# Weight tiles split whole, partial sums put back into PSUM, and wider adaLN tiles in a float32 decoder block

## The chip, the cores and the metric

The kernel runs on one core of one Trainium2 chip. The metric is the device time of one execution in microseconds. A core has TensorE (PE in the profile, with PEld for its weight loads), VectorE (DVE), ScalarE (ACT), GpSimd (POOL), SyncE (SP, which here issues nearly all loads) and 16 DMA engines.

## The reference

One decoder layer over 256 tokens of width 2048, all in float32. What matters of it:

```python
mod = silu(c) @ ada_w + ada_b                    # 2048 -> 6 x 2048
sh1, sc1, g1, sh2, sc2, g2 = split(mod, 6)
h = rms_norm(x, mix_pre_g) * (1 + sc1) + sh1
q, k, v, a, g = split(h @ w_in)                  # 1024 columns each
attn = causal_attention(q, k, v)                 # 8 heads of 128; one block of 256 keys
u = silu(layer_norm(causal_depthwise_conv(a * sigmoid(g), 31 taps)))
y = concat(attn, u) @ w_out
x = x + g1 * rms_norm(y, mix_post_g)
h = rms_norm(x, ffn_pre_g) * (1 + sc2) + sh2
y = (silu(h @ w_gate) * (h @ w_up)) @ w_down     # hidden width 5632
x = x + g2 * rms_norm(y, ffn_post_g)
```

## The kernel before

**Products in three parts.** Every large product is made of fp32r matmuls. A weight tile of 1 MB (4 blocks of 128 rows by 512 columns, name `raw`) is loaded from HBM; ScalarE rounds it into a high tile `wh` (line 610, or 630 where two column groups share a load), and VectorE subtracts that from the tile and keeps the rest as a low tile `wl` (line 611 or 631). The activations exist as a high and a low tensor too, and PE adds three products: high by high, low weight by high, high by low. A `raw` tile is split in two operations of 1024 columns per engine, into tiles of 4 KB per partition, of which there are five high and five low.

**Two forms.** In `multiply_all` (line 656) a job that is `side` (line 668, matmuls on line 674) holds 128 weight columns still and moves 256 token columns, so that its result has channels on partitions. Else (`mm`, lines 680 to 682) 128 tokens are held still, once for each of two token halves `t`, and 512 weight columns move. Before the change the q, k, a and g parts of w_in and all of gate and up are `side`; v, w_out and w_down are not. A unit of PE work is two K blocks of one token half.

**Stages.** `chunks` cuts the 16 K blocks of the first normalisation: for each chunk the adaLN scale and shift (SC1, SH1) are made, `h_chunk` (line 534) turns and scales x into `h0` and `h1`, and then come those w_in products that `cuts` lets end with this chunk. A product cut into parts keeps its sum in SBUF: `put` (line 709) copies the first part out with ScalarE and adds each later part with VectorE (line 717). Then come attention, the convolution (`conv`, line 759; 6 of 8 channel tiles go through ScalarE, lines 786 to 791), a layer norm, w_out in two parts, the second normalisation (`h2_chunk`, line 1113), and the feed-forward part in three passes of 4, 3 and 4 groups of 512 hidden columns. The first pass runs gate and up in four K parts (`fcuts`).

**adaLN.** `ada` (line 453) makes 128 to 512 columns of one of the six vectors from tiles of 1 MB (96 in all), either on PE (line 476, mode 'p'), on VectorE (lines 485 and 487, mode 'd'), or on the one that the plan finds free (mode 'a'). PE then sums over partitions (line 518) or spreads the row (line 512).

**Order.** Nothing is ordered by the chip's arrival order. `Plan` simulates the engines at build time with a cost and a priority (`pri`) for each task and writes the resulting order down, one queue per engine. Loads are picked in `pick_dma` from a queue of weights and a queue of adaLN tiles; the `before` and `after` numbers say at which weight load an adaLN tile must or may go. At most two weight loads whose split isn't done run ahead (`nw`):

```python
if a is not None and (w is None or a["before"] <= w["i"]):
    pick = "a" if a_ok else None
elif w_ok and ahead < nw:
    pick = "w"
elif a_ok and a["after"] <= w["i"]:
    pick = "a"
```

Where PE has nothing to do, the plan gives it small matmuls (line 422) that keep it active. Buffers are named pools: `raw` has 5 tiles of 8 KB, `t2` (512-column scratch) 3, PSUM four banks `pa` for the large products and four banks `pt` for the rest.

## Time and profile before

| | |
|---|---|
| median of 3 runs | 1223.05 us (1222.06 to 1223.63) |
| the profiled execution | 1223.58 us, span 1221.8 us, mean granted clock 0.993 |
| PE busy | 1196.4 us (98% of the span) |
| DVE busy | 877.6 us (72%) |
| ACT busy | 599.7 us (49%) |
| DMA | 307.71 MB, mean 252 GB/s |

The span runs from the first to the last instruction. The time of an execution has a little outside the span. Matmuls are pipelined, so that the length of one in the profile is more than the distance from one to the next; PE's pace is read from the starts.

### The profile page before, as it was taken

How to read it: one execution, taken by the hardware profiler on the slowest of the kernel's cores; microseconds unless marked ns; L12 is line 12 of the kernel's file. 1: busy time of each engine (PE TensorE's matmuls, PEld its weight loads, DVE VectorE, ACT ScalarE, POOL GpSimd, SP SyncE). 2: the span in 40 equal slices, each digit the busy share in tenths (PEclk: the TensorE clock that was granted, in tenths of full speed). 3: DMA queues.
4: the chain of work that ended last, by engine and by line, in shares of the span. 5: the costliest groups of instructions: out<-in, count | busy, mean ns of one | idle time of the engine just before them, and what ended most of it. 6: DMA issues, size and time to landing. Idle time of an engine off the chain costs nothing.

```text
span 1221.8 us, 19898 instructions
## 1 busy us (share of the span) xinstructions
PE 1196.4 (98%) x8275; PEld 1072.2 (88%) x8275; DVE 877.6 (72%) x1121; ACT 599.7 (49%) x860; POOL 16.2 (1%) x29
## 2 busy tenths in 40 slices
PE   5999999999999989999999999999999999999997
PEld 4899799997558769999998789999988999999886
DVE  4799889999978789998788996444555455455554
ACT  3643344998965465534454344434433444444441
POOL 1000000000000010000000000000000000000000
PEclk9999999999998999999999999999999999999999
DMA  9999996558997989988558997655556555555532
GB/s 334 343 341 340 370 348 207 177 179 302 343 383 253 326 315 375 323 297 274 173 185 324 365 363 254 196 174 179 198 175 192 187 173 184 195 173 179 200 104 69
DMA packets 160507, 307.71 MB, mean 252 GB/s; under 512 B 5244, under 2 KB 21920, under 8 KB 159648
## 3 DMA queue, kind: packets, MB, share of 16 engines
q1 hardware_dynamic: 159520, 304.11, 72.5%
q0 software_dynamic: 544, 2.11, 0.5%
q8 instruction: 65, 1.06, 0.4%
q10 hardware_dynamic: 352, 0.21, 0.1%
q14 instruction: 26, 0.21, 0.0%
HBM read 304.32 MB, written 2.10 MB: 251 GB/s over the span
## 4 chain that ended last, share of the span: by engine, by line
PE 89%; ACT 4%; DMA 3%; DVE 1%; issue 1%; SPq 1%; POOL 0%; POOLq 0%; DVEq 0%; ACTq 0%
PE pa L674 54%; PE pa L680 10%; PE pa L682 10%; PE pa L681 10%; PE pt L476 3%; DMA raw<-in_ada_w_dram 2%; ACT prod L788 2%; ACT wh L610 1%; PE pt L518 1%; DMA xt<-in_x_dram 1%; DVE t L487 1%; PE pt L512 1%; SPq L626 0%; DVE wl L611 0%; PE pt L825 0%
## 5 line engine op out<-in xcount | busy, mean ns | idle before, releaser
L674 PE MATMUL pa<-h,wh 128*128 128x256 f32 x3840 | 701.6, 284 | 0.0
L611 DVE TENSOR_TENSOR wl<-raw,wh 128x1024 fp32r<-128x1024 f32 x372 | 451.3, 1223 | 271.8 <-ACT wh L610 270.8
L610 ACT ACTIVATE wh<-raw 128x1024 fp32r<-128x1024 f32 x372 | 392.6, 1060 | 498.0 <-PE pa L674 291.1
L674 PEld LDWEIGHTS pa<-h,wh 128*128 128x128 f32 x3840 | 593.9, 188 | 6.4 <-issue 2.7
L674 PE MATMUL pa<-h,wl 128*128 128x256 f32 x1920 | 540.9, 282 | 0.0
L674 PEld LDWEIGHTS pa<-h,wl 128*128 128x128 f32 x1920 | 363.9, 190 | 0.5 <-issue 0.2
L487 DVE SCALAR_TENSOR_TENSOR t<-raw,cact,t 128x512 f32<-128x512 f32 (+1 forms) x238 | 160.9, 676 | 7.6 <-DVE stats L832 0.3
L680 PE MATMUL pa<-wh,hid 128*128 128x512 f32 x352 | 140.9, 400 | 0.0
L682 PE MATMUL pa<-wh,hid 128*128 128x512 f32 x352 | 139.6, 397 | 0.0
L681 PE MATMUL pa<-wl,hid 128*128 128x512 f32 x352 | 139.6, 397 | 0.0
L681 PEld LDWEIGHTS pa<-wl,hid 128*128 128x128 f32 x352 | 66.4, 189 | 16.5 <-issue 0.7
L680 PEld LDWEIGHTS pa<-wh,hid 128*128 128x128 f32 x352 | 66.4, 189 | 16.5 <-issue 0.7
L682 PEld LDWEIGHTS pa<-wh,hid 128*128 128x128 f32 x352 | 66.4, 189 | 16.1
L788 ACT ACTIVATE prod<-conv,taps 128x256 f32<-128x256 f32 x180 | 74.9, 504 | 0.2 <-DVE conv L791 0.2
L791 DVE TENSOR_TENSOR conv<-conv,prod 128x1536 f32<-128x1536 f32 x30 | 52.6, 1753 | 2.1 <-ACT prod L788 1.9
L476 PE MATMUL pt<-raw,cpad 128*32 128x512 f32 (+1 forms) x384 | 45.7, 571 | 5.5 <-DMA raw<-in_ada_w_dram 5.4
L476 PEld LDWEIGHTS pt<-raw,cpad 128*32 128x32 f32 x384 | 9.1, 114 | 21.7 <-issue 10.0
L680 PE MATMUL pa<-wh,mixa 128*128 128x512 f32 x64 | 28.0, 438 | 0.0
L680 PE MATMUL pa<-wh,h 128*128 128x512 f32 x64 | 26.9, 421 | 0.0
L682 PE MATMUL pa<-wh,mixa 128*128 128x512 f32 x64 | 26.3, 412 | 0.0
L681 PE MATMUL pa<-wl,mixa 128*128 128x512 f32 x64 | 26.3, 410 | 0.0
L774 DVE SCALAR_TENSOR_TENSOR conv<-conv,taps 128x256 f32<-128x256 f32 x60 | 25.7, 480 | 0.0
(154 smaller groups left out, 786.5 us busy)
## 6 DMA issues: line engine op xcount, KB each, us to landing
raw<-in_ada_w_dram SPq DMA_DIRECT2D x96, 1024.0 KB, 7.4
raw<-in_w_gate_dram SPq DMA_DIRECT2D x44, 1024.0 KB, 5.3
raw<-in_w_up_dram SPq DMA_DIRECT2D x44, 1024.0 KB, 5.2
raw<-in_w_down_dram SPq DMA_DIRECT2D x44, 1024.0 KB, 5.1
raw<-in_w_in_dram SPq DMA_DIRECT2D x32, 1024.0 KB, 6.8
raw<-in_w_out_dram SPq DMA_DIRECT2D x16, 1024.0 KB, 7.9
raw<-in_w_in_dram SPq DMA_DIRECT2D x16, 512.0 KB, 7.4
xt<-in_x_dram SPq DMA_DIRECT2D x2, 1024.0 KB, 10.1
```

Of the source, the lines that this page charges most:

```text
L476: nc.tensor.matmul(ps.t[32 * (k % 4):32 * (k % 4) + 32, 0:wd], cpad[:, k0 + k, :], view()[:, k, :], start=me == mine[0] and k < 4, stop=me ...
L487: nc.vector.scalar_tensor_tensor(acc.t[:, 0:wd], view()[:, k, :], s, acc.t[:, 0:wd], op0=ALU.mult, op1=ALU.add)
L512: a = add("PE", 0.86, min(prio, pri["cap"]), lambda: nc.tensor.matmul(pt.t, ones, acc.t, start=True, stop=True), [a], [pt, acc])
L610: a = add("ACT", 0.475 * m, p, lambda raw=raw, u=u, m=m, wh=wh: nc.scalar.activation(wh.t[:, 0:m, :], raw.t[:, u:u + m, :], AF.Copy), [loa ...
L611: b = add("DVE", 0.567 * m, p, lambda raw=raw, u=u, m=m, wh=wh, wl=wl: nc.vector.tensor_sub(wl.t[:, 0:m, :], raw.t[:, u:u + m, :], f32(wh. ...
L674: nc.tensor.matmul(job.ps[t].t[:, 256 * n:256 * n + 256], w.t[:, j, cs], h, start=u == 0 and j == r and n == 0 and i == 0, stop=end and j ...
L680: nc.tensor.matmul(job.ps[t].t, hi, wh.t[:, j, :], start=u == 0 and j == r, stop=False)
L681: nc.tensor.matmul(job.ps[t].t, hi, wl.t[:, j, :], start=False, stop=False)
L682: nc.tensor.matmul(job.ps[t].t, lo, wh.t[:, j, :], start=False, stop=end and j == r + len(ks) - 1)
L774: nc.vector.scalar_tensor_tensor(cacc[:, k, :], upad[:, k, i:i + 256], w, cacc[:, k, :], op0=ALU.mult, op1=ALU.add)
L788: nc.scalar.activation(T("prod")[:, i % 2, k, :], upad[:, k, i:i + 256], AF.Copy, scale=w)
L791: pa = add("DVE", 0.267 * CFG["nact"] + 0.07, pri["conv"] + 0.001 * i, lambda i=i: nc.vector.tensor_add(cacc[:, nv:], cacc[:, nv:], T("pro ...
```

## The change

It has these parts.

- A `raw` tile is split in one operation of up to 2048 columns per engine (`split`), into three high and two low tiles of 8 KB per partition.
- A job that continues a sum in SBUF (`base`) no longer adds behind its matmuls. ScalarE copies the sum back into the job's PSUM bank ahead of them, and they accumulate on it. `put` always copies with ScalarE. The last part of a sum is then used straight from PSUM: the sigmoid and the product of the gated units, SiLU and product of gate and up, the squares and the gain of y.
- Gate and up are no longer `side`. Their product has tokens on partitions, so `up_evac` turns it with four PE transposes per 512 columns and token half.
- adaLN pieces can be 1024 columns wide: a tile of 1 MB then holds 2 K blocks of 1024 columns, and a piece holds two scratch tiles. The pieces are listed in `s2`, `g1` and `g2` and in `chunks`.
- The settings in `CFG` are others: cuts, chunks, modes, priorities, load positions, 5 convolution tiles on ScalarE instead of 6, the second token half of x from weight load 3 on instead of 1.

```diff
 CFG = {'raw': 5,
- 'wh': 5,
- 'wl': 5,
+ 'wh': 3,
+ 'wl': 2,
...
- 'x1_before': 1,
+ 'x1_before': 3,
  'uni': 2,
- 'g1_before': 23,
- 'c_before': (-192, -5, 77, 198),
+ 'g1_before': 126,
...
- 'pri': {'conv': 10.889,
-         'att': 1.269,
-         'g1': 2.484,
-         's2': 2.504,
-         'g2': 8.462,
-         'cap': 1.455,
-         'ln': 2.276,
-         'glu': 6.517,
-         'h': 0.32,
-         'turn': 7.06,
-         'hid': 8.565,
-         'h2': 2.033},
+ 'pri': {'conv': 28.181,
+         'att': 0.346,
+         'g1': 1.434,
+         's2': 7.314,
+         'g2': 2.213,
+         'cap': 0,
+         'ln': 2.918,
+         'glu': 0.2,
+         'h': 0,
+         'hid': 0,
+         'h2': 0.821,
+         'base': 4.302,
+         'turn': 1.115},
  'silu': 1,
- 'h1': 'DADDDADA',
- 'h2': 'DADDAAAA',
+ 'h1': 'DADDADAD',
+ 'h2': 'DAADADDD',
...
- 'nact': 6,
- 'stagger': 4,
- 'stagger1': 4,
- 'joint': 2,
+ 'nact': 5,
+ 'stagger': 7,
+ 'stagger1': 8,
+ 'joint': 1,
...
- 'fcuts': (0, 4, 8, 12, 16),
- 'mode': {1: 'pdap', 0: 'daad', 2: 'papp', 4: 'padd', 3: 'dpdd', 5: 'dddd'},
- 'chunks': (0, 2, 4, 6, 8, 12, 16),
- 'cuts': ((0, 2, 6, 12, 16), (0, 2, 6, 16), (0, 4, 6, 8, 16)),
+ 'fcuts': (0, 4, 8, 16),
+ 'mode': {1: 'pdaa', 0: 'ppdp', 2: 'daap', 4: 'pada', 3: 'paap', 5: 'dadp'},
+ 'chunks': (0, 2, 4, 8, 16),
+ 'cuts': ((0, 2, 4, 8, 16), (0, 4, 8, 16), (0, 8, 16)),
  'parts': ((0, 1, 2, 3), (4, 5, 6), (7, 8, 9, 10)),
- 'g1_from': 51,
- 'c_after': (50, 119, -180, -13),
- 'g2_from': 0}
+ 'g1_from': 1,
+ 'c_after': (-9, 103, -49, 33),
+ 'g2_from': 0,
+ 's2': ((0, 4), (4, 8), (8, 16)),
+ 'g1': ((0, 8), (8, 16)),
+ 'g2': ((0, 8), (8, 16)),
+ 'inj': 1}
...
-    wh_pool = Slots([sbt([P, 2, 512], "wh%d" % i, F32R) for i in range(CFG["wh"])])
-    wl_pool = Slots([sbt([P, 2, 512], "wl%d" % i, F32R) for i in range(CFG["wl"])])
+    wh_pool = Slots([sbt([P, 4, 512], "wh%d" % i, F32R) for i in range(CFG["wh"])])
+    wl_pool = Slots([sbt([P, 4, 512], "wl%d" % i, F32R) for i in range(CFG["wl"])])
...
+        c0, c1 = kbs
         n = c1 - c0
-        wd = P * n
+        mode = CFG["mode"][m][c0 // 4]
+        nc2 = max(1, n // 4)
+        wd = P * min(n, 4)
         per = 16 // n
-        acc = Buf(ac_pool)
+        acc = [Buf(t2_pool) for _ in range(1 if mode == "p" else nc2)]
...
+                    strips = 4 // nc2
                     for k in range(per):
-                        nc.tensor.matmul(ps.t[32 * (k % 4):32 * (k % 4) + 32, 0:wd], cpad[:, k0 + k, :], view()[:, k, :],
-                                         start=me == mine[0] and k < 4, stop=me == mine[-1] and k >= per - 4,
-                                         tile_position=(0, 32 * (k % 4)), skip_group_check=True)
+                        for h in range(nc2):
+                            o = 32 * (k % strips + strips * h)
+                            nc.tensor.matmul(ps.t[o:o + 32, 0:wd], cpad[:, k0 + k, :], view()[:, k, wd * h:wd * h + wd],
+                                             start=me == mine[0] and k < strips, stop=me == mine[-1] and k >= per - strips,
+                                             tile_position=(0, o), skip_group_check=True)
...
+                        for h in range(nc2):
+                            w = view()[:, k, wd * h:wd * h + wd]
+                            if me == mine[0] and k == 0:
+                                nc.vector.tensor_scalar(acc[h].t[:, 0:wd], w, s, None, op0=ALU.mult)
+                            else:
+                                nc.vector.scalar_tensor_tensor(acc[h].t[:, 0:wd], w, s, acc[h].t[:, 0:wd], op0=ALU.mult, op1=ALU.add)
+            dve = 0.2 + 0.178 * per + 0.00111 * per * wd if nc2 == 1 else 2.75
...
+            pts = [Buf(pt_pool) for _ in range(nc2)]
+            o = m * D + P * c0
+            a = plan.fetch(prio, lambda: nc.gpsimd.dma_start(br.t[0:64 * nc2 - 63:64, :], ada_b[:, o:o + P * n].rearrange("o (h n) -> (o h) n", n=512)), [prev], 0.01, [br])
...
+            def spread():
+                for h in range(nc2):
+                    if all_pe() and nc2 == 2:
+                        nc.tensor.matmul(pts[h].t, sel[:, h:h + 1].to_broadcast([P, P]), acc[0].t, start=True, stop=True)
+                    else:
+                        nc.tensor.matmul(pts[h].t, ones, acc[h].t, start=True, stop=True)
+            a = add("DVE", 0.602 * nc2, prio, bias, [a], [br] + acc)
+            a = add("PE", 0.86 * nc2, min(prio, pri["cap"]), spread, [a], pts + acc)
...
+    def split(load, raw, n):
+
+        wh, wl = Buf(wh_pool), Buf(wl_pool)
+        p = 1.0 + 1e-4 * nw[0]
+        a = add("ACT", 0.02 + 0.465 * n, p, lambda: nc.scalar.activation(wh.t[:, 0:n, :], raw.t[:, 0:n, :], AF.Copy), [load], [raw, wh])
+        b = add("DVE", 0.07 + 0.533 * n, p, lambda: nc.vector.tensor_sub(wl.t[:, 0:n, :], raw.t[:, 0:n, :], f32(wh.t[:, 0:n, :])), [a], [raw, wh, wl])
+        plan.queue(load, plan.wq, {"t": load, "i": nw[0], "end": b})
+        nw[0] += 1
+        return wh, wl, b
...
             load = add("DMA", 0.728 * n, 0, fetch, bufs=[raw])
+            wh, wl, b = split(load, raw, n)
             for u in range(0, n, 2):
-                m = min(2, n - u)
...
+                units.append((kbs[i + u:i + min(u + 2, n)], wh, wl, b, range(u, min(u + 2, n))))
...
+        for i, (units, job) in enumerate(pairs):
+            if job.base is not None and CFG["inj"]:
+                for t in range(NT):
+                    place, deps = job.base(t)
+                    last[i][t] = add("ACT", 0.48, pri["base"], lambda job=job, t=t, place=place: nc.scalar.activation(job.ps[t].t, place(), AF.Copy),
+                                     deps + begun[-1], [job.ps[t]])
+            begun.append([])
...
+                loose = job.base is not None and bool(CFG["inj"])
...
                         for i, (w, h) in enumerate(((wh, hi), (wl, hi), (wh, lo))):
-                            nc.tensor.matmul(job.ps[t].t[:, 256 * n:256 * n + 256], w.t[:, j, cs], h, start=u == 0 and j == r and n == 0 and i == 0,
-                                             stop=end and j == r + len(ks) - 1 and n == 1 and i == 2)
...
+            last[i][t] = add("PE", (0.72 if job.side else 0.705) * len(ks), 3.0, side if job.side else mm, deps, [wh, wl, job.ps[t]])
+            if u == 0:
+                begun[base + i].append(last[i][t])
...
-    def put(dst, job, last, first, prio=0.0, more=()):
-
-        last = [[x] + list(more) for x in last]
-        ts = []
-        for t in range(NT):
-            if first:
-                ts.append(add("ACT", 0.48, prio, lambda t=t: nc.scalar.activation(dst(t), job.ps[t].t, AF.Copy), last[t], [job.ps[t]]))
-            else:
-                ts.append(add("DVE", 0.602, prio, lambda t=t: nc.vector.tensor_add(dst(t), dst(t), job.ps[t].t), last[t], [job.ps[t]]))
-        return ts
+    def put(dst, job, last, prio=0.0, more=()):
+
+        return [add("ACT", 0.48, prio, lambda t=t: nc.scalar.activation(dst(t), job.ps[t].t, AF.Copy), [last[t]] + list(more), [job.ps[t]]) for t in range(NT)]
+
+    def base_of(place, made, key):
+
+        if key not in made:
+            return None
+        tasks = made[key]
+        return lambda t: (lambda: place(t), [tasks[t]])
...
         def f(job, last):
-            AGD[kind, j] = put(lambda t: pair(T("ag")[:, kind], 2 * j + t), job, last, first)
-            if fin and kind == 1:
-                glu(j)
+            if not fin:
+                AGD[kind, j] = put(ag_place(kind, j), job, last)
+            elif kind == 1:
+                SIG[j] = [add("ACT", 0.48, pri["glu"], lambda t=t: nc.scalar.activation(ag_place(1, j)(t), job.ps[t].t, AF.Sigmoid), [last[t]], [job.ps[t]]) for t in range(NT)]
+            else:
+                for t in range(NT):
+                    ct = 4 * j + 2 * t
+                    U[ct] = U[ct + 1] = add("DVE", 0.69, pri["glu"], lambda t=t, ct=ct: nc.vector.tensor_mul(
+                        upad[:, ct:ct + 2, HALO:], job.ps[t].t.rearrange("p (k n) -> p k n", k=2), T("ag")[:, 1, ct:ct + 2, :]), [last[t], SIG[j][t]], [job.ps[t]])
         return f
...
+    def y_evac(y, junk, part, cg, fin, base, gdep):
+
+        d = y_place(y, cg)
...
             if not fin:
+                YP[y, cg] = put(d, job, last, more=PVD if y is y1 and part == 0 else ())
...
+                a = add("ACT", 0.61, 0.1, lambda t=t, o=o: nc.scalar.activation(T(junk)[:, t, :], job.ps[t].t, AF.Square, scale=ROOT, accum_out=stats[:, o:o + 1]), [last[t]], [job.ps[t]])
+                b = add("DVE", 0.69, 0.15, lambda t=t: nc.vector.tensor_mul(d(t), job.ps[t].t, gain[:, 512 * cg:512 * cg + 512]), [last[t], gdep[cg]], [job.ps[t]])
...
                 z, ga = GATE[g][t]
...
+                a = add("DVE", 0.69, 0.0, lambda t=t, z=z: nc.vector.tensor_mul(z.t, z.t, job.ps[t].t), [last[t], ga], [job.ps[t], z])
...
+                pt = Buf(pt_pool)
+
+                def turn(z=z, pt=pt):
+                    for k in range(4):
+                        nc.tensor.transpose(pt.t[:, P * k:P * k + P], z.t[:, P * k:P * k + P], ident)
+                a = add("PE", 0.434, pri["turn"], turn, [a], [z, pt])
 
                 def part(s, t=t):
-                    return pair(T("hid%d" % s), 2 * slot + t)
-                h = add("ACT", 0.48, pri["hid"], lambda z=z, part=part: nc.scalar.activation(part(0), z.t, AF.Copy), [a], [z])
-                l = add("DVE", 0.602, pri["hid"], lambda z=z, part=part: nc.vector.tensor_sub(part(1), z.t, f32(part(0))), [h], [z])
+                    return T("hid%d" % s)[:, 4 * slot:4 * slot + 4, P * t:P * t + P]
+                h = add("ACT", 0.48, pri["hid"], lambda pt=pt, part=part: nc.scalar.activation(part(0), pt.t.rearrange("p (k n) -> p k n", k=4), AF.Copy), [a], [pt])
+                l = add("DVE", 0.602, pri["hid"], lambda pt=pt, part=part: nc.vector.tensor_sub(part(1), pt.t.rearrange("p (k n) -> p k n", k=4), f32(part(0))), [h], [pt])
                 HID[slot][t] = [h, l]
+                PARTD.append(last[t])
...
-        return Job(pa_pool, h_stat, h1_deps, (ag_evac if kind >= 3 else qkv_evac)(kind % 3, j, k0 == 0, k1 == KB), kind != 2)
+        evac, place, made = (ag_evac, ag_place, AGD) if kind >= 3 else (qkv_evac, qkv_place, QKV)
+        kind %= 3
+        return Job(pa_pool, h_stat, h1_deps, evac(kind, j, k1 == KB), (evac, kind) != (qkv_evac, 2), base_of(place(kind, j), made, (kind, j)))
...
+        for k0 in range(c0, c1, 4):
+            outs = h_chunk(k0, min(k0 + 4, c1), sd, pri["h"], outs, [(0,), (1,)] if c0 == 0 and CFG["x1_before"] else [(0, 1)])
...
+    G1D = [e for ks in CFG["g1"] for e in ada(G1, ks, n1 + CFG["g1_before"], CFG["g1_from"], pri["g1"], [gl])]
...
+    S2D = []
+    for i, ks in enumerate(CFG["s2"]):
+        at = n1 + nout + 2 * nc_ * (max(x for x in CFG["fcuts"] if x <= ks[0]) // 4)
+        fr = n1 + nout + CFG["c_after"][i]
+        S2D += [[ada(m, ks, at + CFG["c_before"][i], fr, pri["s2"]) for m in (SC2, SH2)]] * ((ks[1] - ks[0]) // 4)
...
         for k0, k1 in zip(fc, fc[1:]) if n0 else ():
...
+                ev = part_evac(i) if k1 < KB else up_evac(g, i // 2) if i % 2 else gate_evac(g)
+                weights(w, 0, 512 * g, list(range(k0, k1)), Job(pa_pool, h2_stat, h2_deps, ev, base=part_base(i)))
...
+            weights(w_gate, 0, 512 * g, list(range(KB)), Job(pa_pool, h2_stat, h2_deps, gate_evac(g)))
+            weights(w_up, 0, 512 * g, list(range(KB)), Job(pa_pool, h2_stat, h2_deps, up_evac(g, slot)))
```

## Rows read from the trace of the kernel before

**Rows 1.** The page: engines, busy us, share of the span, instructions.

```profile
PE 1196.4 (98%) x8275; PEld 1072.2 (88%) x8275; DVE 877.6 (72%) x1121; ACT 599.7 (49%) x860; POOL 16.2 (1%) x29
```

**Rows 2.** The chain that ended last, longest pieces: start us, us, what.

```profile
745.54 125.27 PE pa L674 x1044
...
938.27 184.32 PE pa L674 x1536
```

**Rows 3.** Order of time, all engines, start of the kernel.

```profile
8.82 5.62 SPq L626 DMA_DIRECT2D raw<-in_w_in_dram  x1
...
14.49 0.65 SPq L445 DMA_DIRECT2D xt<-in_x_dram  x1
...
25.81 1.91 ACT L448 ACTIVATE ag<-xt 128x2048 f32<-128x2048 f32 x1 [0.54 <-DMA xt<-in_x_dram]
...
32.66 1.94 PE L476 MATMUL pt<-raw,cpad 128*32 128x256 f32 x16
34.53 0.58 PE L674 MATMUL pa<-h,wh 128*128 128x256 f32 x1
```

**Rows 4.** Stretches: length, busy us of PE, PEld, DVE, ACT, POOL, granted clock, DMA share, GB/s.

```profile
214.00:280.00 66.00, 65.94 (x490) 62.63 (x489) 63.90 (x89) 65.75 (x144) 0.00 (x0) 1.00 0.56 191
280.00:384.00 104.00, 102.91 (x542) 68.20 (x542) 91.81 (x136) 79.12 (x172) 2.18 (x4) 0.97 0.90 323
```

**Rows 5.** Order of time between w_out and gate.

```profile
444.12 0.69 DVE L1142 TENSOR_TENSOR h<-t,h 128x512 fp32r<-128x512 f32 x1
...
448.96 0.37 PE L674 MATMUL pa<-h,wh 128*128 128x256 f32 x1
```

**Rows 6.** Order of time behind the last matmul.

```profile
1212.58 0.69 DVE L717 TENSOR_TENSOR y<-y,pa 128x512 f32<-128x512 f32 x1 [0.19 <-PE pa L682]
1213.31 0.60 ACT L954 ACTIVATE pa<-y 128x512 f32<-128x512 f32 x1 [4.89 <-DVE y L717]
```

**Rows 7.** Order of time, PE: first w_down matmul of the last run, first instruction behind it.

```profile
1122.43 0.40 PE L680 MATMUL pa<-wh,hid 128*128 128x512 f32 x1
...
1212.38 2.17 PE L422 MATMUL pt<-ident 128*128 128x128 f32 x18
```

**Rows 8.** Order of time, PE: four transposes inside the projections, and the next two matmuls.

```profile
36.83 0.60 PE L555 MATMUL pt<-ident,t 128*128 128x128 f32 x4
37.19 0.37 PE L674 MATMUL pa<-h,wh 128*128 128x256 f32 x1
37.39 0.28 PE L674 MATMUL pa<-h,wl 128*128 128x256 f32 x1
```

**Rows 9.** Groups by shape, PE: adaLN products and transposes; busy us, mean ns, idle before.

```profile
L476 PE MATMUL pt<-raw,cpad 128*32 128x512 f32 x272 | 35.6, 604 | 4.3 <-DMA raw<-in_ada_w_dram 4.2
...
L476 PE MATMUL pt<-raw,cpad 128*32 128x256 f32 x112 | 10.1, 491 | 1.2 <-DMA raw<-in_ada_w_dram 1.2
...
L1119 PE MATMUL pt<-ident,t 128*128 128x128 f32 x32 | 4.9, 277 | 0.6 <-ACT t L1115 0.6
```

**Rows 10.** Groups by shape, DVE and then ACT.

```profile
L611 DVE TENSOR_TENSOR wl<-raw,wh 128x1024 fp32r<-128x1024 f32 x372 | 451.3, 1223 | 271.8 <-ACT wh L610 270.8
L487 DVE SCALAR_TENSOR_TENSOR t<-raw,cact,t 128x512 f32<-128x512 f32 x171 | 128.4, 751 | 5.2 <-DVE stats L832 0.3
...
L717 DVE TENSOR_TENSOR part<-part,pa 128x512 f32<-128x512 f32 x36 | 23.8, 682 | 2.1 <-PE pa L674 2.1
...
L1009 DVE TENSOR_TENSOR hid<-t,hid 128x512 fp32r<-128x512 f32 x22 | 14.2, 686 | 0.0
...
L610 ACT ACTIVATE wh<-raw 128x1024 fp32r<-128x1024 f32 x372 | 392.6, 1060 | 498.0 <-PE pa L674 291.1 <-PE pa L682 122.6 <-DMA raw<-in_w_in_dram 26.7
L788 ACT ACTIVATE prod<-conv,taps 128x256 f32<-128x256 f32 x180 | 74.9, 504 | 0.2 <-DVE conv L791 0.2
L1008 ACT ACTIVATE hid<-t 128x512 fp32r<-128x512 f32 x22 | 13.0, 620 | 2.1 <-DVE t L1001 2.1
```

More of the change, by code (lines that the diff above doesn't have):

```diff
@@ new lines, in ada @@
+            a = add("DVE", 0.602 * nc2, prio, bias, [a], [br] + acc)
+            a = add("PE", 0.86 * nc2, min(prio, pri["cap"]), spread, [a], pts + acc)
+            ends = []
+            for h in range(nc2):
+                g = gain[:, P * c0 + 512 * h:P * c0 + 512 * h + 512]
+                ends.append(add("DVE", 0.602, prio, lambda g=g, h=h: nc.vector.tensor_mul(g, g, pts[h].t), [a] + list(deps0), [pts[h]]))
+            return ends
+        pt = Buf(pt_pool)
+        def sums():
+            for j in range(min(n, 4)):
+                if all_pe() and nc2 == 2:
+                    nc.tensor.matmul(pt.t[:, 2 * j:2 * j + 2], acc[0].t[:, P * j:P * j + P], sel, start=True, stop=True)
+                else:
+                    for h in range(nc2):
+                        nc.tensor.matmul(pt.t[:, nc2 * j + h:nc2 * j + h + 1], acc[h].t[:, P * j:P * j + P], ones[:, 0:1], start=True, stop=True)
@@ L521, in fin, with price, cols_ @@
+        def price(t):
+            t.cost = 0.18 * min(n, 4) * (1 if all_pe() else nc2)
+        a = add("PE", 0.72, min(prio, pri["cap"]), sums, [prev], [pt] + acc)
+        a.late = price
         def fin():
-            bias = adab[:, 16 * m + c0:16 * m + c1]
+            def cols_(ap):
+                return ap.rearrange("p (h j) -> p h j", h=nc2)
+            got = pt.t[:, 0:n].rearrange("p (j h) -> p h j", h=nc2)
+            bias = cols_(adab[:, 16 * m + c0:16 * m + c1])
             if m in (SH1, SH2):
@@ L875, in attention @@
         j = h // 4
-        z = Buf(hd_pool)
+        z = Buf(t2_pool)
         o = P * h
@@ L1091, in block_kernel @@
             late = fin and cg >= 4 - CFG["joint"]
-            got = weights(w_out, 0, 512 * cg, list(range(k0, k1)), Job(pa_pool, mix_stat, mix_deps, y_evac(y1, part, cg, fin, 64, G1D)), None if late else 0)
+            got = weights(w_out, 0, 512 * cg, list(range(k0, k1)), Job(pa_pool, mix_stat, mix_deps, y_evac(y1, "junk1", part, cg, fin, 64, G1D), base=y_base(y1, cg)), None if late else 0)
             if late:
```

228 lines of the change are left out of this document (86 added, 142 removed).

## Prediction

> **What bounds the kernel now.** I read the table of engines first: TensorE (PE) is busy 98% of the span, VectorE (DVE) 72%, ScalarE (ACT) 49% [rows 1]. A busy PE isn't yet a PE without gaps, so next came the chain that ended last. Its longest pieces are PE at gate and up matmuls: 1044 of them in 125.27 us and 1536 in 184.32 us, 120.0 ns from one to the next in both [rows 2]. For these stretches nothing but PE's own list counts. The order of time then shows where PE loses anything: in the first 34.5 us, before the first projection matmul [rows 3]; a little between 280 and 384 us, where DMA moves 323 GB/s after 191 GB/s in the stretch before, so that loads are late there that an idle queue could have fetched earlier [rows 4]; between w_out and the first gate matmul at 448.96 us [rows 5]; and behind the last matmul [rows 6]. The rest is PE's work. So I price the change by what it does to PE's list and to these four places, and ask of ACT and DVE only whether they stay hidden. The profiled execution took 1223.58 us for a span of 1221.8 us; the median of the runs is 1223.05 us, 0.5 us less. The sum is made against 1223.6.
>
> **1. Gate and up change form.** They lose the sideways form (weights stationary, 256 token columns moving) for the form of w_down (tokens stationary, 512 weight columns moving). 11 groups x 2 weights x 16 K blocks x 2 token halves x 6 = 4224 matmuls of 256 columns become 2112 of 512. The old ones cost 120.0 ns each: 506.9 us. The price of the new ones is that of the last w_down run: 384 matmuls (4 column groups x 16 blocks x 2 x 3) from 1122.43 to 1212.38 us, 234.2 ns each [rows 7]: 494.7 us. The change saves 12.2 us.
> The Trainium skill ("TensorE: Matmul & The Clock Gate", Back-to-back issue gap) has a lone matmul take columns / 2.4 GHz plus 2.5 ns, so 109.2 and 215.8 ns; by it the exchange would save 461.3 - 455.8 = 5.5 us and the whole sum would be 6.7 us worse. The trace has both forms, at 120.0 and 234.2 ns, and I go by it.
>
> **2. The hidden layer must now be turned.** Its product comes out with tokens on partitions, and w_down wants hidden channels there: 22 new groups of four transposes. Four such transposes inside the projections start at 36.83 us and the next matmul at 37.19 us; it holds PE a further 0.2 us instead of 0.12 us, so 0.36 + 0.08 = 0.44 us a group [rows 8]: 9.7 us. The other end is the 277 ns that the record of one transpose shows [rows 9]: 88 x 0.277 = 24.4 us, if none overlapped. I take 9.7, since those are the same work at the same place in PE's queue.
> The Trainium skill ("TensorE: Matmul & The Clock Gate", Part 4: PE-mode transpose) gives about 275 ns for a transpose in a kernel; with 88 x 0.275 = 24.2 us the change would be 14.5 us dearer than I have it. It agrees with the length of the records (277 ns), not with their distance.
>
> **3. adaLN tiles.** 96 tiles of 1 MB remain. Before, PE took 34 tiles of 512-column products (272 instructions, two for each, four products a tile) and 7 of 256 columns (112 instructions, eight products a tile) [rows 9]; one holds PE about 1.03 us (35.6 / 34 = 1.05 us of records). Counted from the mode letters, after the change 12 wide and 8 narrow tiles are PE's ('p'), 44 DVE's ('d'), and 32 wide ones go to whoever is free ('a'). Ends: no 'a' on PE, (12 - 34) x 1.03 + 1.03 = -21.6 us; all of them, +11.3 us. Before, 13 of 20 'a' tiles fell to PE. DVE gets emptier (part 4), so I take 18 of 32: 30 wide and 8 narrow, -3.1 us.
>
> **4. Splits and partial sums, off the path.** The operations of 1024 columns, 372 on line 610 (1060 ns) and 372 on line 611 (1223 ns) with 4 and 4 on lines 630 and 631, become 188 and 188 of 2048. By the line through 512 columns (620 and 686 ns) and 1024, 2048 columns cost 1.94 us on ACT and 2.30 us on DVE [rows 10]: ACT saves 34 us, DVE 28 us. The adds of line 717 leave DVE: 126 in five groups like the one shown, 0.682 us each, 86 us. ACT gets 98 copies back into PSUM and 58 more copies out, counted over the new cuts, at 0.62 us at most: 97 us, less 31 of line 788's pieces, 16 us. ACT goes from 600 to some 647 us of 1222 and DVE from 878 to some 770; both are hidden under PE (1196 us) on average. A copy into PSUM waits at a low priority in ACT's queue; behind it waits the first matmul of its job, and ahead of it can stand a split (1.94 us) or five convolution pieces (2.5 us). It may start when the job before has begun, 5.6 us ahead (4 blocks x 2 x 3 x 0.234). I price all this at nothing; without the cover it is rival B.
>
> **5. Start.** The second token half of x moves in SP's queue behind the second w_in load. Now it is issued at 14.49 us, behind one load that waited in the queue from 8.82 us for 5.62 us; it has landed when its squares begin at 25.81 us, and the first projection matmul comes at 34.53 us, right after an adaLN tile that began at 32.66 us [rows 3]. One more megabyte ahead of it, 1.05 MB at the 323 GB/s of a full queue [rows 4], is 3.2 us; PE can put an adaLN tile into part of it. Ends 0 and +3.2; I take +2.5. Behind it, the cuts (0, 4, ...) give PE less early work (4 groups instead of 7 after the first chunk), which its next adaLN chunk just covers by my count; no price.
>
> **6. From w_out to gate.** The first gate matmul waits today for both token halves; in the new form for its own. Half 0 is ready when line 1142 ends, 444.12 + 0.69 = 444.81 us; the matmul comes at 448.96 us [rows 5]. Up to 4.2 us, though PE does adaLN work in part of it; the add ahead of the squares goes too. Ends 0 and -4.9 (with the add's 0.7 us of part 7); I take -3.0.
>
> **7. Tail.** The last add (1212.58) to the square behind it (1213.31) drops out: -0.7 us [rows 6].
>
> **8. Middle.** G1's tiles may now load from the first weight on, so into the 191 GB/s stretch, and DVE there, 63.90 of 66 us [rows 4], loses adds. On the other side stand two low tiles instead of five half as large. I take -2, ends -6 and +6.
>
> Sum: -12.2 + 9.7 - 3.1 + 2.5 - 3.0 - 0.7 - 2.0 = -8.8, so **1214.8 us**. With every end taken the good way it would be 1187.9 (-12.2 + 9.7 - 21.6 - 4.9 - 0.7 - 6), with every end the bad way 1255.6 (-12.2 + 24.4 + 11.3 + 3.2 - 0.7 + 6); neither is likely as a whole.
>
> **Rivals.**
> **A, the forecast:** PE stays the bound and its list gets shorter; 1208 to 1220, 0.54.
> **B, the low tiles become the bound (slower).** A low tile comes free when PE is through with the tile before last, and PE then works 24 x 0.234 = 5.6 us on the next. DVE needs 2.3 us of that for the subtraction, so it may be 3.3 us late, where five half tiles left four of them (11 us). Between 214 and 384 us DVE has 63.90 of 66 and 91.81 of 104 us of work [rows 4], and an adaLN tile there is four products of 751 ns [rows 10], 3.0 us in one piece. Two such pieces ahead make the subtraction 2.7 us late (6.0 - 3.3), and PE stands. The stretch of 170 us has room for at most 30 tiles; from 4 late ones on, the gain is gone, and with 9 the time is 1239. For it: DVE's fullness. Against it: DVE loses a tenth of its work. 0.20.
> **C, no gain:** more 'a' tiles stay with PE, 25 of 32 instead of 18: 7 x 1.03 = 7.2 us more, 1222. For it: 13 of 20 did so before, and in the new settings PE puts them ahead of its matmuls. Against it: DVE lacks work more often. 0.12.
> **D, DVE takes most 'a' tiles:** 4 on PE instead of 18, 14.4 us less: 1200. For it: DVE's lost 108 us of work. Against it: PE can take a tile after each piece of two blocks (1.4 us), DVE only when it has nothing else. 0.09.
> **E, nothing gained by the form:** a 512-column matmul costs as much as two of 256, 240.0 ns; part 1 falls away, 1227.0. The two streams stand against it [rows 2, 7], though they come from different stages. 0.02. The Trainium skill's rule in part 1 lies between this and the forecast, at 1221.5.
> **F, the transposes don't overlap:** 88 x 0.277 us instead of 9.7; 1229.5. The length of their records is for it [rows 9], their distance against it [rows 8]. 0.03. The Trainium skill's figure in part 2 is this case.
>
> **How the numbers follow.** A change within 0.2% (2.4 us) can't be told from none. A and D are faster: 0.63. C is the same: 0.12. B, E and F are slower: 0.25. The time is A's, 1215. For 8 in 10, the range reaches to D's 1200 below and above over C to E and F and the lower part of B, to 1230. A's own range is 1208 to 1220.
>
> **What would show it.** Right: no 128x256 matmuls at gate and up, 2112 more of 512 columns about 234 ns apart, long pieces of the chain made of them; 88 more transposes with a 0.4 us gap to the next matmul; DVE near 770 us, ACT near 650; the first gate matmul soon after half 0 is ready. Wrong: PE waits put down to DVE's subtraction or to ACT's copy into PSUM, at tile distance (5.6 us), above all from 214 to 384 us (B); over 40 wide adaLN tiles on PE (C) or under 20 (D); a first projection matmul later than 38 us. My weakest step is the share of 'a' tiles, then the two low tiles.

## The result, and the profile after

The changed kernel takes **1212.32 us** (median of 4 runs, 1209.03 to 1214.31) where the kernel before has 1223.34 beside it (4 runs): a ratio of 0.9909, 95% interval 0.9885 to 0.9933. The forecast was 1215, between 1200 and 1230. The profiled execution is the fastest of the four, 1209.03 us for a span of 1207.3.

The table of engines, then the groups of instructions of VectorE, ScalarE and TensorE that answer to [rows 1, 9, 10] (count, busy us, mean ns, idle before):

```profile
PE 1179.0 (98%) x6219; PEld 970.4 (80%) x6219; DVE 787.2 (65%) x832; ACT 632.0 (52%) x787; POOL 13.0 (1%) x25
```

```profile
L643 DVE TENSOR_TENSOR wl<-raw,wh 128x2048 fp32r<-128x2048 f32 x188 | 430.5, 2290 | 297.5 <-PE pa L726 262.7 <-PE pa L718 9.9 <-ACT wh L642 9.4
...
L505 DVE SCALAR_TENSOR_TENSOR t<-raw,cact,t 128x512 f32<-128x512 f32 x235 | 161.7, 747 | 3.8 <-DMA raw<-in_ada_w_dram 3.0
```

```profile
L642 ACT ACTIVATE wh<-raw 128x2048 fp32r<-128x2048 f32 x188 | 360.8, 1919 | 368.4 <-PE pa L727 282.9 <-DMA raw<-in_w_in_dram 23.1 <-DMA raw<-in_w_down_dram 22.5
```

```profile
L492 PE MATMUL pt<-raw,cpad 128*32 128x512 f32 (+1 forms) x328 | 37.4, 560 | 5.3 <-DMA raw<-in_ada_w_dram 5.2
...
L1067 PE MATMUL pt<-ident,t 128*128 128x128 f32 x88 | 13.2, 272 | 0.0
```

One group of the new transposes in the order of time, with the two products behind it:

```profile
559.43 0.60 PE L1067 MATMUL pt<-ident,t 128*128 128x128 f32 x4
559.78 0.48 PE L725 MATMUL pa<-wh,h 128*128 128x512 f32 x1
560.10 0.40 PE L726 MATMUL pa<-wl,h 128*128 128x512 f32 x1
```

PE is still busy 98% of a span that is 14.5 us shorter. VectorE lost 90 us, ScalarE gained 32. The split operations cost 2290 and 1919 ns (I had 2.30 and 1.94 us). Of the 328 adaLN records on PE, 200 are wide, 25 tiles, where 34 were; so 13 of the 32 'a' tiles fell to PE, not 18. The group of transposes holds PE for 0.35 us and the product behind it for 0.32 us instead of 0.23: 0.44 us a group, as forecast.

The windows that answer to [rows 4], and the order of time at the places of [rows 3, 5, 6]:

```profile
214.00:280.00 66.00, 65.42 (x457) 45.47 (x456) 64.41 (x99) 57.75 (x122) 0.55 (x1) 1.00 0.99 370
280.00:384.00 104.00, 103.80 (x589) 90.01 (x589) 93.73 (x136) 91.31 (x173) 0.72 (x1) 0.98 0.50 169
```

```profile
30.77 1.93 PE L492 MATMUL pt<-raw,cpad 128*32 128x256 f32 x16 [4.20 <-DMA raw<-in_ada_w_dram]
...
36.74 0.36 PE L718 MATMUL pa<-h,wh 128*128 128x256 f32 x1
```

```profile
426.18 0.95 PE L560 MATMUL pt<-ones,t 128*128 128x1 f32 x8
...
437.71 1.11 PE L1181 MATMUL pt<-ident,t 128*128 128x128 f32 x4 [3.31 <-ACT t L1177]
...
439.33 0.77 PE L725 MATMUL pa<-wh,h 128*128 128x512 f32 x1
```

```profile
1198.64 1.95 PE L429 MATMUL pt<-ident 128*128 128x128 f32 x16
1198.90 0.60 ACT L1014 ACTIVATE junk<-pa 128x512 f32<-128x512 f32 x1 [4.89 <-PE pa L727]
```

In the middle PE works 103.80 of 104 us (102.91 before) while DMA moves 169 GB/s there and 370 in the stretch ahead: the loads went into the old idle queue. The first projection matmul is 2.2 us later than [rows 3], the first gate matmul 9.6 us earlier than [rows 5]. From the end of w_out to gate there are 13.2 us (426.18 to 439.33); before it was 14.6, from this instruction on to [rows 5]:

```profile
434.36 1.06 PE L476 MATMUL pt<-raw,cpad 128*32 128x512 f32 x8
```

The tail is 0.8 us shorter.

PE's order of time gives this account of several executions (us). "Projections" reaches from the first projection matmul to the first w_out matmul, "w_out" to the start of what follows its last one, "gap" to the first gate matmul, "rest" to PE's end. "adaLN" is PE's time start to start on these tiles before gate.

```
                        first  projections  w_out   gap    rest   adaLN
before                  34.5      268.2     131.6   14.6   765.6   46.3
before, 32 B moved e6   34.0      269.1     129.9   14.7   758.4   47.4
 + form alone      e8   32.7      266.6     128.2   11.1   763.1   44.5
changed, half tiles e4  38.3      280.2     108.6   10.6   761.5   39.0
changed            e1   35.8      282.6     105.4   13.6   761.5   36.1
changed, sideways  e2   35.9      282.6     105.2   18.2   760.8   34.9
changed, h +64 B  e11   36.2      277.0     105.9   13.5   753.2   36.4
```

### The profile page after: what moved, and what is told of

The parts are those of the page before. It is cut to its first block, busy times and chain, and to the rows that moved or that the text cites. A ratio compares the mean times of both kernels' runs of the same rounds, so it can differ in the third digit from the quotient of the medians.

```text
span 1207.3 us, 15349 instructions
## 1 busy us (share of the span) xinstructions
PE 1179.0 (98%) x6219; PEld 970.4 (80%) x6219; DVE 787.2 (65%) x832; ACT 632.0 (52%) x787; POOL 13.0 (1%) x25
## 4 chain that ended last, share of the span: by engine, by line
PE 88%; DVE 4%; DMA 4%; ACT 2%; issue 1%; POOL 0%; SPq 0%; DVEq 0%; POOLq 0%; ACTq 0%
PE pa L726 23%; PE pa L725 23%; PE pa L727 23%; PE pa L718 14%; DMA raw<-in_ada_w_dram 4%; DVE wl L643 1%; PE pt L492 1%; PE pt L560 1%; DVE t L505 1%; PE pt L1067 1%; DVE conv L827 1%; ACT prod L841 0%; DVE conv L844 0%; POOL stats L446 0%; PE pt L429 0%
## 5 line engine op out<-in xcount | busy, mean ns | idle before, releaser
L643 DVE TENSOR_TENSOR wl<-raw,wh 128x2048 fp32r<-128x2048 f32 x188 | 430.5, 2290 | 297.5 <-PE pa L726 262.7
L642 ACT ACTIVATE wh<-raw 128x2048 fp32r<-128x2048 f32 x188 | 360.8, 1919 | 368.4 <-PE pa L727 282.9
L725 PE MATMUL pa<-wh,h 128*128 128x512 f32 x768 | 307.5, 400 | 0.0
L726 PE MATMUL pa<-wl,h 128*128 128x512 f32 x768 | 303.5, 395 | 0.0
L727 PE MATMUL pa<-wh,h 128*128 128x512 f32 x768 | 303.5, 395 | 0.0
L718 PE MATMUL pa<-h,wh 128*128 128x256 f32 x1024 | 189.4, 284 | 1.0 <-ACT pa L702 1.0
L725 PEld LDWEIGHTS pa<-wh,h 128*128 128x128 f32 x768 | 144.9, 189 | 35.1 <-issue 2.8
L727 PEld LDWEIGHTS pa<-wh,h 128*128 128x128 f32 x768 | 144.9, 189 | 34.0
L718 PEld LDWEIGHTS pa<-h,wh 128*128 128x128 f32 x1024 | 159.3, 188 | 9.1 <-issue 5.0
L505 DVE SCALAR_TENSOR_TENSOR t<-raw,cact,t 128x512 f32<-128x512 f32 x235 | 161.7, 747 | 3.8 <-DMA raw<-in_ada_w_dram 3.0
L718 PE MATMUL pa<-h,wl 128*128 128x256 f32 x512 | 144.3, 282 | 1.1 <-DVE wl L643 1.1
L718 PEld LDWEIGHTS pa<-h,wl 128*128 128x128 f32 x512 | 96.4, 188 | 1.4 <-DVE wl L643 1.3
## 6 DMA issues: line engine op xcount, KB each, us to landing
xt<-in_x_dram SPq DMA_DIRECT2D x2, 1024.0 KB, 11.1
```

The source lines that it names most:

```text
L505: nc.vector.scalar_tensor_tensor(acc[h].t[:, 0:wd], w, s, acc[h].t[:, 0:wd], op0=ALU.mult, op1=ALU.add)
L642: a = add("ACT", 0.02 + 0.465 * n, p, lambda: nc.scalar.activation(wh.t[:, 0:n, :], raw.t[:, 0:n, :], AF.Copy), [load], [raw, wh])
L643: b = add("DVE", 0.07 + 0.533 * n, p, lambda: nc.vector.tensor_sub(wl.t[:, 0:n, :], raw.t[:, 0:n, :], f32(wh.t[:, 0:n, :])), [a], [raw, wh ...
L718: nc.tensor.matmul(job.ps[t].t[:, 256 * n:256 * n + 256], w.t[:, j, cs], h, start=not loose and u == 0 and kb == ks[0] and n == 0 and i == ...
L725: nc.tensor.matmul(job.ps[t].t, hi, wh.t[:, j, :], start=not loose and u == 0 and kb == ks[0], stop=False, skip_group_check=loose)
L726: nc.tensor.matmul(job.ps[t].t, hi, wl.t[:, j, :], start=False, stop=False, skip_group_check=loose)
```

## The experiments

Theory T, as I held it: PE's list is the bound and got shorter by the form and the adaLN tiles. Against it: R1, the larger split operations give the gain; R2, the partial sums in PSUM; R3, only the new order. Later came theory A, on where tiles lie in SBUF. Ratios are against the kernel before on the same chip; us are medians. The account above is of single profiled executions, so differences of a us or two in it can be one execution's.

**e1, the changed kernel again.** No edit.

> The changed kernel, unaltered, beside the kernel before. It settles nothing between the theories; it gives a second profile and the scatter of the changed kernel, whose four runs so far lie between 1209.0 and 1214.3 us where the kernel before has 1222.1 to 1223.9. Every theory expects 1209 to 1214 us. If the scatter is the program's own, the second profile shows the same instruction counts as the first and longer waits or a lower granted clock somewhere.

1208.15 us, 0.9879 (0.9862 to 0.9897). Among these runs the slower ones have the lower mean clock (1207.27 us at 0.997, 1211.70 at 0.993); among the four first runs the fastest has the lowest, 0.991. These windows (columns as in [rows 4]) are of the two profiled executions of the same program, the first run's and e1's:

```profile
28.00:38.00 10.00, 7.23 (x54) 4.54 (x55) 3.04 (x6) 3.91 (x7) 1.49 (x3) 0.66 1.10 350
362.00:374.00 12.00, 12.00 (x65) 10.48 (x64) 4.97 (x10) 5.48 (x9) 0.72 (x1) 0.86 0.25 87
432.00:444.00 12.00, 8.21 (x42) 6.61 (x35) 7.02 (x15) 6.98 (x13) 3.67 (x2) 0.72 0.99 381
```

```profile
28.00:38.00 10.00, 7.16 (x80) 5.44 (x83) 5.23 (x9) 5.40 (x9) 2.02 (x3) 1.00 1.10 350
362.00:374.00 12.00, 12.00 (x72) 10.50 (x71) 6.52 (x11) 7.25 (x12) 0.72 (x1) 1.00 0.23 78
432.00:444.00 12.00, 8.55 (x44) 7.35 (x45) 6.40 (x13) 7.33 (x13) 3.67 (x2) 0.86 0.81 316
```

At three places the granted clock drops to 0.50, the lower level of 1.2 GHz, for some us: at about 30 and 436 us, where PE waits, and at about 368, behind 32 one-column products (L878). At which of them it drops differs between executions of one program. PE's 512-column products start 0.43 us apart there (368.27, 368.70, 369.13 us in the first run) instead of 0.23. One minus the clock, times the window, is the most that can be lost: 8.4 us in the first, 1.7 in e1. PE waits in part of these windows, and the two spans differ by only 1.8 us (1207.3 and 1205.5).

**e2, gate and up sideways again.**

```
-  Job(pa_pool, h2_stat, h2_deps, gate_evac(g))         # and up, and the parts
+  Job(pa_pool, h2_stat, h2_deps, gate_evac(g), True)
-  for k in range(4): nc.tensor.transpose(pt.t[:, P*k:P*k+P], z.t[:, P*k:P*k+P], ident)
```

> The changed kernel with one part undone: the gate and up products go back to the sideways form (1024 and 512 columns, the hidden tile comes out with its features on the partitions) and the transposes of the hidden tile go. Everything else, the settings of the order too, stays. Theory T (TensorE's list is the bound and became shorter; the form gives 12.2 us and the transposes cost 7.8) expects 4.4 us more than the changed kernel, and as much as 7.4 if the transposes hide behind weight loads better than I read: 1216 to 1219 us where the changed kernel is at 1212. The rivals that give the whole gain to the larger split operations (R1), to the partial sums in PSUM (R2) or to the new order alone (R3) expect no difference, 1211 to 1213. Slower by 10 us or more would mean that the transposes cost nothing.

1213.89 us, 0.9922 (0.9906 to 0.9939): 5.7 us more than e1, as T had it, but not where T had it. The rest from the first gate matmul on is 0.8 us shorter than e1's. The gap is 4.6 us longer:

```profile
423.69 0.94 PE L560 MATMUL pt<-ones,t 128*128 128x1 f32 x8
...
439.32 2.91 PE L429 MATMUL pt<-ident 128*128 128x128 f32 x12
441.88 0.56 PE L718 MATMUL pa<-h,wh 128*128 128x256 f32 x1
```

In sideways form gate waits for both token halves, and the granted clock over 432 to 444 us is 0.57 (e1: 0.86), so even what PE does there takes longer.

**e3, the form alone, in the kernel before.** The opposite edit, and the due time of the transposes.

> The kernel before with one part of the change alone: gate and up products with 512 columns and the four transposes for each hidden tile; 4 KB split tiles, partial sums in SBUF, adaLN spans and settings of the order as before but for the due time of the transposes. Theory T expects 1223.3 - 12.2 + 7.8 = 1219 us, down to 1216 if the transposes overlap better. R1, R2 and R3 expect 1223 us or slower.

1219.80 us, 0.9970 (0.9953 to 0.9987). The same picture: rest 766.3 (before 765.6), gap 11.1 (before 14.6). Neither e2 nor e3 leaves the whole gain to R1, R2 or R3, which expected no gain from the form.

**e4, half tiles.**

```
- 'wh': 3, 'wl': 2,        sbt([P, 4, 512], "wh%d" % i, F32R)   # wl too; one operation of 2048
+ 'wh': 5, 'wl': 5,        sbt([P, 2, 512], "wh%d" % i, F32R)   # two operations of 1024
```

> The changed kernel with the split tiles of before: five high and five low tiles of 4 KB, each filled by an operation of 1024 columns, in place of three and two of 8 KB filled by operations of 2048; the rest, the order's settings too, is that of the changed kernel. The split then takes about 28 us more of VectorE and 34 us more of ScalarE. Theory T expects this hidden: 1212 to 1214 us, a part of it because the order may put an adaLN tile more on TensorE (about 1 us each). R1 (the larger operations and the whole tiles give the gain) expects 1218 us or more.

**1205.22 us**, 0.9852 (0.9833 to 0.9871): 3 us faster than e1, with intervals that just overlap. R1 has the wrong sign, and T missed it. The gap is 10.6 us instead of 13.6; in the same two profiles e4's projections are 2.4 us shorter and its w_out is 3.2 us longer, with a mean clock of 0.83 from 360 to 380 us where e1's is 1.00. In e1, POOL's operation on one column, VectorE's beside it, ScalarE's behind it, and PE:

```profile
432.22 3.13 POOL L446 TENSOR_TENSOR stats<-stats,mhalf 128x1 f32<-128x1 f32 x1 [4.20 <-DVE stats L441]
```

```profile
432.06 2.28 DVE L643 TENSOR_TENSOR wl<-raw,wh 128x2048 fp32r<-128x2048 f32 x1
434.26 0.68 DVE L1204 TENSOR_TENSOR h<-t,h 128x512 fp32r<-128x512 f32 x1
```

```profile
435.38 0.72 ACT L1177 ACTIVATE t<-x,stats 128x512 f32<-128x512 f32 x1 [2.58 <-POOL stats L446]
```

```profile
436.16 0.66 PE L1181 MATMUL pt<-ident,t 128*128 128x128 f32 x4 [3.32 <-ACT t L1177]
```

and POOL's in e4, the first while VectorE splits 1024 columns (428.61, 1.22 us), the second without a split beside it:

```profile
428.77 1.46 POOL L446 TENSOR_TENSOR stats<-stats,mhalf 128x1 f32<-128x1 f32 x1 [0.69 <-DVE stats L441]
434.42 0.55 POOL L446 TENSOR_TENSOR stats<-stats,mhalf 128x1 f32<-128x1 f32 x1 [4.19 <-DVE stats L441]
```

POOL needs 0.55 us alone and, beside VectorE's operations, ends 0.4 us after the last of them that reads two tiles of SBUF: in e1 behind the split and the subtraction of line 1204, 3.13 us. The inverse root that POOL takes holds up ScalarE's scaling of the second token half; PE, in whose queue that half's transposes (L1181) stand ahead of gate, waits 3.32 us. The Trainium skill ("SBUF — State Buffer", Who interferes with whom) says that a VectorE instruction with two SBUF inputs contends with a GpSimd instruction that reads SBUF; these rows agree. e4's order has no split at this root at all, so the two runs don't show what the length alone does, and that this wait is the 3 us between them is argued.

**e5 to e8, where the tiles lie.** Between the families of before and after, a 512-column product of the last w_down pass costs 234.2 and 232.4 ns (e1 below, 240 products), and so it is, within 1 ns, in the whole of each run.

```profile
1121.61 0.39 PE L725 MATMUL pa<-wh,hid 128*128 128x512 f32 x1
...
1177.38 0.39 PE L725 MATMUL pa<-wh,hid 128*128 128x512 f32 x1
```

The allocator's list shows a difference that I hadn't priced: the change adds an 8-byte tile `sel`, which moves all large tiles behind it by 32 bytes. The edit is one unused tile ahead of them (in e7 one ahead of wh and one behind wl):

```
+    sbt([P, 8], "pad")
     s1, b1, s2, b2 = (sbt([P, KB], n) for n in ("s1", "b1", "s2", "b2"))
```

> The changed kernel with one unused tile of 32 bytes for each partition allocated ahead of the large tiles, so that the tiles that hold the normalized activations, the mixer's halves and the hidden tiles (h0, h1, h2, mixa, mixc, hid) again begin 32 bytes behind a multiple of 64, as in the kernel before; in the changed kernel the new two-column tile sel had moved them onto a multiple of 64. No instruction differs. Read from the traces so far: a 512-column product starts 232.4 ns after the last one in every run of the changed kernel's family and 234.2 ns in the two runs of the family of before. Theory A (the 64-byte boundary of the activations' tiles sets this) expects 234.2 ns again, 3744 x 1.8 = 6.7 us, and 1 us or so for the 256-column products: 1215 to 1216 us where the changed kernel has 1208. Rival (the price comes from the partial sums in PSUM, from VectorE's lighter load or from the instruction stream) expects 232.4 ns and 1208 us.

> The kernel before with the same unused tile of 32 bytes, which moves the activations' tiles onto a multiple of 64. No instruction differs. Theory A expects the 512-column product at 232.4 ns (1632 x 1.8 = 2.9 us) and the 256-column one about 1 ns cheaper (5760, up to 6 us): 1214 to 1220 us where the kernel before has 1223. The rival expects 1223 us and 234.2 ns.

> The changed kernel with two unused tiles of 32 bytes, one ahead of the split weight tiles and one behind them: the high and low weight tiles (the moving operand of the 512-column products, the stationary one of the 256-column ones) now begin 32 bytes behind a multiple of 64, and the activations' tiles stay on a multiple of 64. Theory A in the form that only the stationary operand's place counts expects 232.4 ns for 512 columns and 1208 us, at most 1 to 2 us more from the 256-column products; in the form that the moving operand's place counts it expects 234.2 ns and 1215 us.

> The kernel before with the gate/up form alone, and with the unused tile of 32 bytes that moves the activations' tiles onto a multiple of 64. Theory A expects 3744 x 1.8 = 6.7 us and about 1 us for the 256-column products less than the form alone has at 1219.8: 1211 to 1213 us. Against the kernel before with the same unused tile it shows what the form is worth where the boundary is equal: between -2 and +1 us, since the products of gate, up and down lose 8 us and the transposes cost 7.8. The rival expects 1219 to 1220 us.

e5 1212.53 us, 0.9908 (0.9888 to 0.9928). **e6 1215.53, 0.9944** (0.9925 to 0.9963). e7 1211.46, 0.9912 (0.9894 to 0.9931). e8 1211.30, 0.9907 (0.9888 to 0.9925). Two rows of the order of time of e6 with 240 products between them, then of e5:

```profile
1136.85 0.40 PE L681 MATMUL pa<-wh,hid 128*128 128x512 f32 x1
...
1192.63 0.40 PE L681 MATMUL pa<-wh,hid 128*128 128x512 f32 x1
```

```profile
1136.73 0.39 PE L726 MATMUL pa<-wh,hid 128*128 128x512 f32 x1
...
1192.73 0.39 PE L726 MATMUL pa<-wh,hid 128*128 128x512 f32 x1
```

(1192.63 - 1136.85) / 240 = 232.4 ns, against 234.2 in [rows 7]: the kernel before, with no instruction changed, takes the price of the changed one and 0.56% less time. Its gate and up products of 256 columns go from 120.0 to 118.7 ns. e5 has 233.3, so the move back costs only half of what I expected: 3.5 us by the ratios of e5 and e1. e7 has 233.3 too, which neither form of theory A had. e8 keeps 232.4 and has the time that A gave it; against e6 the form is worth 4.2 us, more than the 2 that I allowed.

**e9, eight adaLN tiles to PE by hand.**

```
- 5: 'dadp'
+ 5: 'padp'
```

> The changed kernel with eight wide adaLN tiles of the last gate vector (G2), which VectorE multiplies during the gate and up products, given to TensorE by hand; nothing else is set otherwise. Theory T (TensorE's list is the bound from the first gate product on, so each adaLN tile given to or taken from it counts in full) expects 8 tiles x 8 records x 0.12 to 0.13 us = 8 us more: 1216 us where the changed kernel has 1208 (1215 to 1217). A rival in which the adaLN products hide in gaps of TensorE expects no difference.

1221.37 us, 0.9992 (0.9980 to 1.0004), 13 more than e1. The new group, in the first w_down pass (632 to 737 us):

```profile
L492 PE MATMUL pt<-raw,cpad 128*32 128x512 f32 x64 | 8.5, 605 | 1.4 <-DMA raw<-in_ada_w_dram 1.4
```

The rest is 9.1 us longer than e1's (770.6), about T's 8; a further 5.3 us lie ahead of gate, where this profile can have lost up to 5 us more to the low clock than e1's. Over the runs the mean clock is 0.9929 (e1 0.9948), which is at most 2 of the medians' 4 us beyond the tiles; the other 2 are open.

**e10, partial sums back in SBUF.**

```
-  'inj': 1      # ScalarE puts the sum back into PSUM
+  'inj': 0      # nc.vector.tensor_add(place(), place(), job.ps[t].t), evacuations read place()
```

with due times and placing letters set anew (`pri`, `c_before`, `c_after`, `g1_before`, `g1_from`, `h1`, `h2`).

> The changed kernel with one part undone: the partial K sums stay in SBUF and VectorE adds each new product to them there, as in the kernel before, in place of ScalarE putting them back into PSUM; the evacuations then read SBUF. Without new settings the order puts the adaLN spans badly, so the due times and the placing letters were set anew for this structure. VectorE gets about 67 us more. If the sums in PSUM are worth nothing on the path, 1208 to 1212 us; my theory has them hidden from the first gate product on but not in the stretch of 80 to 350 us, where VectorE is busy 0.93 to 0.99 of the time and a third of these additions lie: 1213 to 1230 us. R2 (the sums are the main gain) expects 1223 us or more with TensorE's product prices unchanged.

1239.06 us, 1.0133 (1.0115 to 1.0152). PE's longest wait (us in total, times, longest), the VectorE products in one piece that it waits for, and the engines' work from 80 to 350 us here and in e1:

```profile
PE pt L561 <- DVE t L506: 9.3, 2, 7.0
```

```profile
141.95 15.98 DVE L506 SCALAR_TENSOR_TENSOR t<-raw,cact,t 128x512 f32<-128x512 f32 x24
```

```profile
80.00:350.00 270.00, 258.95 (x1896) 227.70 (x1896) 244.34 (x332) 152.04 (x245) 0.55 (x1) 0.98 0.86 310
```

```profile
80.00:350.00 270.00, 269.22 (x1918) 236.49 (x1918) 255.78 (x345) 204.82 (x348) 0.55 (x1) 1.00 0.87 320
```

The projections take 309.3 us (e1 282.6), the rest 764.0 (761.5). With whole tiles and sums in SBUF, PE once waits 7.0 us for VectorE's adaLN work. But VectorE is less busy from 80 to 350 us than in e1 (244.3 against 255.8 us), and so is PE (259.0 against 269.2): a VectorE that is full, as I expected, isn't what the rows show. How much of the 31 us is the sums and how much a poorer order, this run can't tell. It doesn't make R2 the cause of the gain: e8, with the sums in SBUF and half tiles, has 1211.3.

**e11, the activations' tiles 64 bytes on.** As e5, with `sbt([P, 16], "pad")`.

> The changed kernel with one unused tile of 64 bytes for each partition ahead of the large tiles: the activations' tiles move from a multiple of 512 bytes to 64 behind a multiple of 128, the weight tiles stay. No instruction differs. So far: activations on a multiple of 64 and of 512, weights on a multiple of 64: 232.4 ns for a 512-column product; activations 32 behind it: 233.3 (changed kernel) and 234.2 (before, 32 short of a multiple of 512); weights 32 off and activations moved by 64 as well: 233.3. If a multiple of 64 is enough for the activations, this run has 232.4 ns and 1208 us, and the 0.9 ns of the run with shifted weights belong to the weights. If the activations want a multiple of 128 or more, it has 233.3 ns and 1211 us.

**1193.41 us, 0.9753** (0.9740 to 0.9766), outside both expectations and the fastest of all:

```profile
1117.87 0.39 PE L726 MATMUL pa<-wh,hid 128*128 128x512 f32 x1
...
1172.80 0.39 PE L726 MATMUL pa<-wh,hid 128*128 128x512 f32 x1
```

228.9 ns a product, and the 256-column ones about 114 instead of 119. Theory A's rule of 64 bytes has fallen; that the place counts has not. What fits the prices is the distance of the two operands' places modulo 128 bytes: 96 in before, 234.2; 32 in e5 and in e7, 233.3; 0 in e1 and e6, 232.4; 64 here. e7 has its activations at e11's place and its weights 32 bytes on, and 233.3 instead of 228.9 ns, so the weights' place counts too. The distance is only argued: four distances, and e1 has 233.3 itself between 550 and 700 us, e10 in most of its time from 600 us on, with the tiles where e1 has them. The 256-column products don't follow it either: in the projections e5's take 117.3 to 118.7 ns and e1's 118.6 to 120.0.

**e12, half tiles with the order set anew.** e4 with new due times, letters, modes and cuts.

> The version that the runs so far point to: the changed kernel with five high and five low tiles of 4 KB and operations of 1024 columns, which ran at 1205.2 us, with the due times, the placing letters and the cuts of the order set anew for it. The order it gets has about 34 adaLN tiles on TensorE, as the changed kernel. Theory T expects 1198 to 1206 us: the products are the same and only waits ahead of the first gate product can go. If the new order gives a new wait there, 1205 to 1212.

1203.69 us, 0.9845 (0.9831 to 0.9859), beside e4 at 0.9852: no difference. The gap is 5.3 us, but the projections take 287.1. Half tiles together with e11's place weren't tried.

## Why the prediction was right, and where it was right by luck

One part at a time, in ratios to before: the 32 bytes 0.9944 (e6), the form 0.9907 (e8), everything else but the tile size 0.9852 (e4), the whole tiles 0.9879 (e1). In us of 1223: -6.8, -4.5, -6.7, +3.3, together -14.8, which is e1's gain. By the intervals of the ratios each difference is uncertain by 2 to 3 us. The first run's gain was 11.0 us, with lower clocks (mean 0.9925, e1's five runs 0.9948). My -8.8 has the sign and most of the size, from terms that were partly others. Without the place of the tiles the steps make -8.0. In it -4.5 stands against the -5.5 of parts 1, 2 and 6, -6.7 against the -3.3 of parts 3, 5, 7 and 8, and +3.3 against nothing; that the last two errors cancel, and that the place didn't carry the time out of the range, is luck.

- **Not in the sum: the place of the tiles, -6.8 us.** The largest single piece of the gain in this order is a side effect of `sel`; taken back in the changed kernel (e5) it is 3.5 us, at another distance. I took the prices of both forms out of one kernel and carried them to another. For part 1 that is a small error: at e6's 118.7 and 232.4 ns the exchange is worth 10.6 us instead of 12.2. But it moves every product.
- **1 and 2, form and transposes.** Forecast -12.2 + 9.7. PE's products from gate on got 6.3 (e6 to e8), 8.0 (e2 to e1) and 10.1 us (before to e3) shorter; the 88 transposes cost 7.8 to 8.4 by their starts, and 9.6 to 9.7, the forecast, with the longer hold of the product behind each group. With a few more small PE instructions nothing is left: the rest is 0.7 us longer (e3) and 0.8 longer (e1). Rival E's result, by way of the transposes and not of the price. From e6 to e8 it is 4.7 longer, 1.7 of it low clock (0.77 over the first 7.3 us of gate).
- **3, the adaLN share, mis-sized.** Forecast -3.1 with 18 'a' tiles on PE. 13 went there, and PE's time on these tiles fell by 10.2 us (46.3 to 36.1), 6.8 of it without the whole tiles (45.8, with 1.2 behind gate in e8, to 39.0 in e4), about the 6.7 us of that step. That T's list counts there is shown by e9; that the whole step is this term is argued. The step also holds the sums in PSUM and the new settings, and no run has the new order alone, so R3 stays open for these 6.7 us.
- **4, splits and sums at nothing.** Failed for the whole tiles, +3.3 us: hidden on average, but the 2048-column split stands beside POOL's root at a place where nothing covers it, and there the gap is 3.0 us longer. That the gap is the cause is argued (e4). I looked at the queues of VectorE and ScalarE and not at POOL. For the sums e10 leaves a price between 0 and 31 us. VectorE came to 787 us instead of 770, and five more adaLN tiles at 3.0 us are most of that; ScalarE came to 632 instead of 647.
- **5, start.** Forecast +2.5, measured +2.2 in the first run, +1.3 in e1. In the first run the squares of the second token half begin at 27.80 us instead of 25.81, as the longer queue ahead of them has it.
- **6, w_out to gate.** Forecast -3.0; the form gives 3.5 (e3, e8) to 4.6 us (e2), the only place where it pays by a mechanism that I can name, and e1's gap is 3 us above e4's: 14.6 to 13.2 in all. e3 and e8 also start the projections 1.3 to 1.8 us earlier, with 0.9 us less of adaLN on PE ahead of them; the form itself doesn't explain that.
- **7, 8.** The tail got 0.8 us shorter (forecast 0.7). PE's idle time from 280 to 384 us fell from 1.1 to 0.2 us; I had 2 us for the middle.
- **Rivals.** B fell: from 214 to 384 us PE has no waits at tile distance, and two low tiles cost what part 4 says, elsewhere. C fell with 13 tiles, D got part of its way. F fell: in a group the transposes start 109 ns apart, though each record shows 272.
